# Four tiles' scores in one run, a state tile for each tile, earlier transposes in the second pass, and values before gates in the last head

## The chip, the core and the metric

The kernel runs on one NeuronCore of a Trainium2 chip. The core has a matrix engine (TensorE; PE in the profile, with its weight loads shown apart as PEld), a vector engine (VectorE, DVE), an activation engine (ScalarE, ACT), a general engine (GpSimd, POOL), and a queue that mainly issues DMAs (SyncE, SP). Each runs its own list of instructions in order, and semaphores hold an instruction back until what it needs is there. The working memory (SBUF) holds the operands; TensorE's products go to PSUM, eight banks of 128 x 512 fp32 values.

The metric is the device time of one execution in microseconds, the median over several runs. The kernel before takes 2855.21 us (three runs, 2853.53 to 2857.36).

## What is computed

One layer of a hybrid trunk: a bidirectional gated linear recurrence (HGRN2, 8 heads of 128 x 128 state, 2048 latent tokens, 256 context tokens), then a gated ConvFFN of width 2816. Both are pre-RMSNorm with adaLN. Cut to the part around the change:

```python
def hgrn2_chunk_scan(q, k, v, logf, s0):
    # S_t = diag(f_t) S_{t-1} + k_t v_t^T,  o_t = S_t^T q_t, in chunks of 64
    b = jnp.cumsum(logf, axis=3)
    qe = q * jnp.exp(b - b_ref)
    ke = k * jnp.exp(b_ref - b)
    scores = jnp.where(mask, jnp.einsum('bhnik,bhnjk->bhnij', qe, ke), 0.0)
    o_intra = jnp.einsum('bhnij,bhnjv->bhniv', scores, v)
    kv = jnp.einsum('bhnjk,bhnjv->bhnkv', k * jnp.exp(b_last - b), v)
    s_final, s_start = lax.scan(step, s0, (decay, kv))      # s <- decay * s + kv
    o_inter = jnp.einsum('bhnik,bhnkv->bhniv', q * jnp.exp(b), s_start)
    return o_intra + o_inter, s_final

def hgrn2_mixer(h_ctx, h_lat, w_in, lb, g_gain, w_out, need_ctx):
    # columns of w_in: q | f_fwd | f_bwd | i (values) | g (output gate)
    for d in range(2):                       # both directions, from the context's final state
        oc_d, s_ctx = hgrn2_chunk_scan(..., s0)
        ol_d, _ = hgrn2_chunk_scan(..., s_ctx)
        o_l = o_l + _flip(ol_d, d, 2)
    return (rmsnorm(o_l, g_gain) * jax.nn.silu(g)) @ w_out

lat = lat + g1 * hgrn2_mixer(...)
lat = lat + g2 * conv_ffn(modulate(rmsnorm(lat, norm_g[1]), sh2, sc2), ...)
return rmsnorm(lat, final_g)
```

## The kernel before

**Precision.** A projection is made of three float32r products: each operand is split into a high and a low part (`split`, L76: ScalarE copies the high part, VectorE subtracts), and `acc` (L327) adds high*high, high*low and low*high over the eight blocks of the inner dimension.

**Start.** The adaLN rows for shift and scale come from 64 products with `w_ada` (L202). Their sums are copied to `m2` (L209), two tiles in the pair of places called `raw`, which the loads of weights share, and transposed (L213). Then the first tiles of tokens are modulated and transposed.

**The scan** (`mixer_scan`, L265). Tokens are taken in two halves `g` of 8 tiles of 128; within a half each of the 8 heads is one call of `head(g, h)` (L617), and in it two units `u` of UT = 4 tiles. For each unit there are five projections of 128 x 512 into a tile `z` (three PSUM banks in turn): two gates, the query, the values, the output gate. `gates`, `swish` and `factors` (L361 to L455) turn them into the factors of the recurrence: `kd`, `sd`, `ke`, `qp`, `qi`, `qm`, `km`. `unit_steps` (L496) then gives the rest of the work of a unit:

- `scores(p)`, for the pair p of tiles: transposes of `kd` (`turned`, into the one bank `tr`, copied to `kt` by ScalarE), 24 small products a tile into a bank of `scs`, then two predicated copies and an add on VectorE, to `at`. Each small fp32 product shows as two instructions in the profile, and so does each transposed or 128-column fp32 product of kv and o.
- `outputs(p, v)`: products `kv` of four (L537), products `o` (L543) of the state `Sf` and of `at`, and between them VectorE steps `Sf` to the next tile (L544). So the second tile's product with the state follows a step that itself follows the first tile's product. ScalarE copies `o` and `kv` out, and DMAs put them to DRAM (`stash`) for the backward direction.

The order of this work is written by hand: a clock ticks once for each inner block of a projection (`tick`, L323), three products long, called a slot here, and `at(when, f)` (L313) hangs work onto a later slot, between the products of projections. The lists of numbers in `head` (L655 to L678) are such distances. `head0`'s weights, the context's projections and `make_tok` (the transposes of the next token tiles) use the same clock. Calls give each instruction its priority; the order on an engine is then made by a planner, which may let a later instruction pass one whose inputs it expects late.

In the last half `ada_rest` also makes four adaLN rows on VectorE, one step every 16 slots, and in its last head `gate1` (L603) loads the gate row `g1`, and `out_weight(k)` (L608) loads a block of `w_out`, scales it, and splits it to places 0 to 3, which hold the tokens of the second half until then: places 0 and 1 those of unit 0, places 2 and 3 those of unit 1. Blocks 0 to 3 are made behind out_gate(0), blocks 4 to 7 behind the last head (L703).

**Memory.** SBUF is full. By the sizes of the tiles in the order of the pools, the low end holds the constants, `raw`, `Sf` and `Sb`, the four places, the weights `w`, and then `cxt` (the context's tokens, not used in the second half) from 118.9 to 135.3 KB. The tiles of the second pass grow from the other end, and the lowest of them is `og`, 117.6 to 134.0 KB, then `ghl` and `kq` above it. A tile can be written when the tiles that lay in its place are no longer read.

**The second pass** (`mixer_out`, L846) goes through the tiles backwards. `heads(t)` (L863) loads `kq` of a tile (and uses `og`, loaded by `load_stash(1, t)`), makes the products `oi` with the backward state `Sb` (L877), adds them to o, steps `Sb` (L886) and normalizes by head (L889 to L896). `heads_T(t)` (L899) transposes the result (L906), multiplies by the gate (L908) and splits it to `ghl`. `residual(n, ...)` (L912) multiplies by `w_out`, half of the columns at a time (24 products, 5.5 us), and `norm2` (L948) normalizes the new latents and puts them to DRAM for the FFN. For tile t the loop at L990 calls `heads(t-2)`, `residual(0)` of t, `heads_T(t-1)`, `load_stash(1, t-3)`, `residual(1)` of t and `norm2(t+1)`. `og` and `kq` hold two tiles each, by the tile's parity.

Of the kernel before, what the change touches and what calls it, by code (L numbers as in the profile page):

```python
# [21 lines left out]
D = 1024  # L22
# [23 lines left out]
def body(ctx, tc, a, out):  # L46
# [93 lines left out]
    cxt = hq.tile([128, 2, 2, 2, 4, 128], F32R, name="cxt")  # L140
# [40 lines left out]
    with ExitStack() as c0:  # L181
# [25 lines left out]
        m2 = [rawp.tile([2, 2, 512], F32, name="m2", tag="raw") for _ in range(2)]  # L207
        for n in range(4):
            ada_done = act.activation(m2[n // 2][:, n % 2], mps[n], AF.Copy)  # L209
        m2f = [m.rearrange("p a b -> p (a b)") for m in m2]  # L210
        mt = p0s.tile([128, 16, 2], F32, name="mt")
        for j in range(16):
            pe.transpose(mt[:, j, :], m2f[j // 8][:, j % 8 * 128:(j % 8 + 1) * 128],  # L213
                         ident[0:2, 0:2])
# [50 lines left out]
    def mixer_scan():  # L265
# [19 lines left out]
        for i in range(2):  # L285
            pool.memset(mb[64 * i:64 * i + 64, 0, 64 - 64 * i:128 - 64 * i], 1.0)
        mfu, mbu = [m.bitcast(U32).to_broadcast([128, 2, 128]) for m in (mf, mb)]
        scs = [ps.tile([128, 2, 2, 128], F32, name=f"sc{i}", tag=f"sc{i}", bufs=1)
               for i in range(2)]
        for sc in scs:  # L290
# [5 lines left out]
        ABs = [[fix.tile([128, 2, 128], F32, name=f"AB{i}{d}") for d in range(2)]  # L296
               for i in range(2)]

        TBs = [fix.tile([128, 4, UT, 4], F32, name=f"TB{i}") for i in range(2)]
        TXs = [fix.tile([128, 2, UT, 4], F32, name=f"TX{i}") for i in range(2)]  # L300
        for i in range(2):
# [3 lines left out]
            for d in range(2):  # L305
                pool.memset(ABs[i][d], 0.0)
        count = {"A": 0}
# [68 lines left out]
        def factors(h, u, t0, q):  # L376
# [60 lines left out]
            qm, km = [mid(n, (UT, 4, 32)) for n in ("qm", "km")]  # L437
# [58 lines left out]
        def unit_steps(h, t0, made):  # L496

            kd, sd, ke, qp, qi, qm, km = made
            kts, ats = {}, {}

            def scores(p):

                kts[p] = turned(kd, 2 * p, 2)
                n = count["A"] % 2
                count["A"] += 1
                sc = scs[n]

                def score(i, d, k, kc, q, qc):
                    pe.matmul(sc[32 * kc:32 * kc + 32, i, d, 32 * qc.start:32 * qc.stop], k, q,
                              start=True, stop=True, skip_group_check=True)  # L510

                for i in range(2):
                    s = 2 * p + i
                    for j in range(4):
                        qc = slice(2 - j // 2 * 2, 4 - j // 2 * 2)
                        score(i, 0, km[:, s, j], j, qm[:, s, qc], qc)
                    for d in range(2):
                        for j in range(4):
                            qc = slice(j // 2 * 2, j // 2 * 2 + 2) if j % 2 == 1 - d \
                                else slice(j, j + 1)  # L520
                            score(i, d, ke[:, d, 4 * s + j], j,
                                  qp[:, d, 4 * s + qc.start:4 * s + qc.stop], qc)
                at_ = gp.tile([128, 2, 128], F32, name="at", tag="at", bufs=2)
                af, ab = ABs[n]
                dve.copy_predicated(af, mbu, sc[:, :, 0])
                dve.copy_predicated(ab, mfu, sc[:, :, 1])
# [1000 lines left out]
```

## Time and profile before

| | us |
|---|---|
| median of three runs | 2855.21 |
| profiled execution | 2855.47 |
| its span, first to last instruction | 2853.8 |
| TensorE busy in it | 2764.3 |
| VectorE busy | 1988.9 |
| ScalarE busy | 1158.9 |
| GpSimd busy | 574.6 |

The profile is that of one execution. Times in it count from the start of its span, and are in us unless marked ns. A row of the timeline has start, duration, engine, line of the kernel, operation, output and inputs by the program's names, array size and shape, and the number of instructions merged in it; in brackets is how long the engine had stood idle before and what released it. A row of busy time by stretch has the stretch, its length, then for PE, PEld, DVE, ACT and POOL the busy time and number of instructions, then TensorE's granted clock as a share of the full one, the share of the DMA engines, and GB/s. Matmuls overlap one another, so the distance of their starts tells more than their durations, and a merged row of several can end behind the start of the next row. A row of waits has who waited for whom, the total, how many times, the longest.

### The profile page before, as it was taken

The page shows a single profiled execution, that of the slowest core. Times are in us where ns is not written, and L with a number is a line of the kernel's source. Part 1 is how long each engine was busy: PE and PEld are TensorE (multiplying, and loading weights), DVE is VectorE, ACT ScalarE, POOL GpSimd, SP SyncE. Part 2 cuts the span into 40 slices and gives each one's busy share as a digit, 9 for nine tenths or more (in the row PEclk, how much of TensorE's full clock was granted, in tenths as well). Part 3 has the DMA queues.
Part 4 walks back from the last instruction along what each step waited for, and adds up shares of the span by engine and source line. Part 5 has one row for each costly group of instructions (what it writes and reads, how often), then busy time and mean ns, then how long its engine had stood idle before and what let it go on. Part 6 is the DMA issues. An engine that isn't in the chain of part 4 may idle for free.

```text
span 2853.8 us, 41978 instructions
## 1 busy us (share of the span) xinstructions
PE 2764.3 (97%) x16072; PEld 2277.4 (80%) x16072; DVE 1988.9 (70%) x2900; ACT 1158.9 (41%) x1910; POOL 574.6 (20%) x884
## 2 busy tenths in 40 slices
PE   7999999999999999997999899999999999999999
PEld 3788888888888788886777688888888888878887
DVE  3666555656665666566887787777887777577887
ACT  5524344332232333333565444444444444333343
POOL 2111111111111111111111243433443332000001
PEclk8999999999999999998999999999999999999999
DMA  5213233223532433226778522225422223887663
GB/s 222 66 53 100 82 101 112 82 63 112 170 111 68 141 85 108 89 74 227 265 263 293 223 95 69 82 86 193 179 89 89 85 71 113 305 297 250 205 196 122
DMA packets 223777, 402.18 MB, mean 141 GB/s; under 512 B 29012, under 2 KB 136404, under 8 KB 217816
## 3 DMA queue, kind: packets, MB, share of 16 engines
q1 hardware_dynamic: 220552, 391.24, 41.5%
q10 hardware_dynamic: 3024, 8.26, 0.7%
q8 instruction: 126, 2.06, 0.3%
q14 instruction: 75, 0.61, 0.1%
HBM read 289.04 MB, written 110.38 MB: 140 GB/s over the span
## 4 chain that ended last, share of the span: by engine, by line
PE 71%; DMA 11%; DVE 11%; ACT 3%; issue 2%; POOL 2%; SPq 0%; DVEq 0%; POOLq 0%; ACTq 0%
PE z L332 9%; PE z L334 9%; PE z L333 9%; PE y L1359 3%; PE y L1357 3%; PE y L1358 3%; PE zd L759 3%; PE zc L759 3%; PE zc L761 3%; PE zd L761 3%; PE zd L762 3%; PE zc L762 3%; PE za L761 3%; PE za L762 3%; PE za L759 3%
## 5 line engine op out<-in xcount | busy, mean ns | idle before, releaser
L332 PE MATMUL z<-tok,w 128*128 128x512 f32 x1280 | 516.7, 404 | 0.1
L333 PE MATMUL z<-tok,w 128*128 128x512 f32 x1280 | 505.1, 395 | 0.0
L334 PE MATMUL z<-tok,w 128*128 128x512 f32 x1280 | 501.8, 392 | 0.3 <-DVE w L78 0.3
L78 DVE TENSOR_TENSOR w<-raw,w 128x512 fp32r<-128x512 f32 (+1 forms) x260 | 239.3, 924 | 88.3 <-ACT w L77 86.1
L332 PEld LDWEIGHTS z<-tok,w 128*128 128x128 f32 x1280 | 241.3, 189 | 49.7 <-issue 2.6
L334 PEld LDWEIGHTS z<-tok,w 128*128 128x128 f32 x1280 | 240.9, 188 | 50.0 <-DVE w L78 0.6
L333 PEld LDWEIGHTS z<-tok,w 128*128 128x128 f32 x1280 | 241.6, 189 | 44.3
L77 ACT ACTIVATE w<-raw 128x512 fp32r<-128x512 f32 (+1 forms) x260 | 195.9, 760 | 177.4 <-PE zd L762 77.4
L1357 PE MATMUL y<-wd,mh 128*128 128x512 f32 x600 | 234.9, 392 | 2.8 <-ACT X L1392 2.8
L1359 PE MATMUL y<-wd,ml 128*128 128x512 f32 x600 | 234.6, 391 | 0.6 <-DVE ml L78 0.5
L1358 PE MATMUL y<-wd,mh 128*128 128x512 f32 x600 | 234.4, 391 | 0.0
L78 DVE TENSOR_TENSOR w<-s,w 128x512 fp32r<-128x512 f32 x126 | 121.2, 967 | 53.9 <-ACT w L77 53.1
L759 PE MATMUL zc<-rT,w 128*128 128x512 f32 x352 | 137.1, 390 | 1.2 <-DVE uv L1244 1.0
L762 PE MATMUL zc<-rT,w 128*128 128x512 f32 x352 | 137.0, 389 | 0.0
L761 PE MATMUL zc<-rT,w 128*128 128x512 f32 x352 | 136.9, 389 | 0.0
L1357 PEld LDWEIGHTS y<-wd,mh 128*128 128x128 f32 x600 | 113.3, 189 | 27.2 <-ACT X L1392 3.7
L385 DVE TENSOR_TENSOR_SCAN S<-F,d 128x528 f32<-128x528 f32 (+1 forms) x80 | 91.5, 1144 | 62.2 <-ACT F L368 62.1
L77 ACT ACTIVATE w<-s 128x512 fp32r<-128x512 f32 x126 | 78.2, 627 | 138.8 <-POOL s L815 81.8
L1359 PEld LDWEIGHTS y<-wd,ml 128*128 128x128 f32 x600 | 113.2, 189 | 25.3 <-DVE ml L78 1.4
L1358 PEld LDWEIGHTS y<-wd,mh 128*128 128x128 f32 x600 | 113.3, 189 | 23.4
L759 PE MATMUL za<-rB,w 128*128 128x512 f32 x336 | 130.7, 389 | 0.0
L761 PE MATMUL za<-rB,w 128*128 128x512 f32 x336 | 130.7, 389 | 0.0
(316 smaller groups left out, 6250.5 us busy)
## 6 DMA issues: line engine op xcount, KB each, us to landing
raw<-in_w_up_dram SPq DMA_DIRECT2D x88, 512.0 KB, 3.8
raw<-in_w_in_dram SPq DMA_DIRECT2D x80, 512.0 KB, 3.9
lr<-m SPq DMA_DIRECT2D x49, 512.0 KB, 5.7
m<-r SPq DMA_DIRECT2D x66, 256.0 KB, 4.1
raw<-in_w_ada_dram SPq DMA_DIRECT2D x32, 512.0 KB, 3.7
kq<-stash SPq DMA_DIRECT2D x15, 1024.0 KB, 8.2
og<-stash SPq DMA_DIRECT2D x15, 1024.0 KB, 6.4
u<-in_w_down_dram SPq DMA_DIRECT2D x51, 256.0 KB, 4.0
```

The lines of the kernel that those rows point to most:

```text
L77: act.activation(h, src, AF.Copy)
L78: dve.tensor_tensor(l, src, h.bitcast(F32), OP.subtract)
L332: pe.matmul(z, w[:, 0, k], h, start=k == 0, stop=False, skip_group_check=True)
L333: pe.matmul(z, w[:, 0, k], l, start=False, stop=False, skip_group_check=True)
L334: pe.matmul(z, w[:, 1, k], h, start=False, stop=k == KT - 1, skip_group_check=True)
L385: dve.tensor_tensor_scan(flat(S[:, d]), flat(F[:, d]), flat(d1[:, 0:ns]), 0.0, OP.mult, OP.max)
L759: pe.matmul(o, w[:, 0, k], r[:, :, 0, k], start=start and k == 0, stop=False, skip_group_check=True)
L761: pe.matmul(o, w[:, 0, k], r[:, :, 1, k], start=False, stop=False, skip_group_check=True)
L762: pe.matmul(o, w[:, 1, k], r[:, :, 0, k], start=False, stop=k == 3, skip_group_check=True)
L1357: pe.matmul(z, lh, rh, start=start, stop=False, skip_group_check=True)
L1358: pe.matmul(z, lh, rl, start=False, stop=False, skip_group_check=True)
L1359: pe.matmul(z, ll, rh, start=False, stop=stop, skip_group_check=True)
```

## The change

It has these parts.

1. `m2` at the start goes to four tiles in the places of `q` and `g` instead of the pair `raw`.
2. `scores` takes all four tiles of a unit in one run: one bank of `scs` for each direction instead of one for each pair, masks and sums over four tiles, transposes of the first pair ahead of the products and of the second pair behind them. `at` is four tiles wide. `qm` and `km` get one buffer each instead of two.
3. `outputs(p, v)` becomes `stepped(p)` (kv, the step of the state into a tile `states` for each of the tiles, the stores of kv) and `outputs(p)` (the products o from these states, their stores). They are called as `stepped(0)`, then `outputs(0)` with `stepped(1)`, then `outputs(1)`.
4. The distances in `head` change: scores 16 and 14 slots behind the query (before 20 and 28, and 22 and 28), the three steps at 5, 9, 13 slots behind the values (before two at 6 and 10, or 10 and 16).
5. In the last head the values of unit 1 come ahead of the output gate of unit 0; `gate1` moves from slot 20 to slot 4; blocks 4 to 7 of `w_out` are loaded and scaled at slots 16 to 28 of that head into `wraw`, in the place of `cxt`, and split behind it.
6. In the second pass `heads_T(t-1)` is called ahead of `heads(t-2)` for tiles 14 to 1; tile 15 keeps the old order.

```diff
-        m2 = [rawp.tile([2, 2, 512], F32, name="m2", tag="raw") for _ in range(2)]
+        m2 = [gp.tile([2, 512], F32, name="m2", tag="qg"[n // 2], bufs=2) for n in range(4)]
         for n in range(4):
-            ada_done = act.activation(m2[n // 2][:, n % 2], mps[n], AF.Copy)
+            ada_done = act.activation(m2[n], mps[n], AF.Copy)
...
-        scs = [ps.tile([128, 2, 2, 128], F32, name=f"sc{i}", tag=f"sc{i}", bufs=1)
-               for i in range(2)]
+        scs = [ps.tile([128, UT, 128], F32, name=f"sc{d}", tag=f"sc{d}", bufs=1)
+               for d in range(2)]
...
-            qm, km = [mid(n, (UT, 4, 32)) for n in ("qm", "km")]
+            qm, km = [mid(n, (UT, 4, 32), bufs=1) for n in ("qm", "km")]
...
+            kts, states, vs = [], [], []
+            at_ = gp.tile([128, UT, 128], F32, name="at", tag="at", bufs=2)
+            q_ = act if h == NH - 1 and t0 == NT - UT else sp
+
+            def scores():
+
+                def score(d, s, k, kc, q, qc):
+                    pe.matmul(scs[d][32 * kc:32 * kc + 32, s, 32 * qc.start:32 * qc.stop], k, q,
                               start=True, stop=True, skip_group_check=True)
 
+                kts.append(turned(kd, 0, 2))
+                for s in range(UT):
                     for j in range(4):
                         qc = slice(2 - j // 2 * 2, 4 - j // 2 * 2)
+                        score(0, s, km[:, s, j], j, qm[:, s, qc], qc)
                     for d in range(2):
                         for j in range(4):
                             qc = slice(j // 2 * 2, j // 2 * 2 + 2) if j % 2 == 1 - d \
                                 else slice(j, j + 1)
+                            score(d, s, ke[:, d, 4 * s + j], j,
                                   qp[:, d, 4 * s + qc.start:4 * s + qc.stop], qc)
+                kts.append(turned(kd, 2, 2))
+                for d in range(2):
+                    dve.copy_predicated(ABs[d], masks[d], scs[d])
+                dve.tensor_tensor(at_, *ABs, OP.add)
+
+            def stepped(p):
+
+                if p == 0:
+                    states.append(gp.tile([128, UT - 1, 128], F32, name="states", tag="states",
+                                          bufs=1))
+                kt, v = kts[p], vs[0]
+                st = [Sf[:, h]] + [states[0][:, i] for i in range(UT - 1)] + [Sf[:, h]]
                 kv = ps.tile([128, 2, 2, 128], F32, name="kv", tag="kv")
                 for d in (1, 0):
                     for i in range(2):
+                        pe.matmul(kv[:, d, i], kt[:, i, d], v[:, 2 * p + i], start=True, stop=True)
                 for i in range(2):
+                    s = 2 * p + i
+                    dve.scalar_tensor_tensor(st[s + 1], st[s], sd[:, 1, s:s + 1], kv[:, 1, i],
                                              OP.mult, OP.add)
                 sk = gp.tile([128, 2, 128], F32, name="sk", tag="sk", bufs=2)
...
+            def outputs(p):
+                v = vs[0]
+                st = [Sf[:, h]] + [states[0][:, i] for i in range(UT - 1)]
+                o = ps.tile([128, 2, 128], F32, name="o", tag="o")
+                for i in range(2):
+                    s = 2 * p + i
+                    pe.matmul(o[:, i], qi[:, 1, 4 * s:4 * s + 4], st[s], start=True, stop=False)
+                    pe.matmul(o[:, i], at_[:, s], v[:, s], start=False, stop=True)
+                so = gp.tile([128, 2, 128], F32, name="so", tag="so", bufs=2)
...
+            def second():
+                outputs(0)
+                stepped(1)
+
+            return scores, (vs.append, lambda: stepped(0), second, lambda: outputs(1))
...
         def out_weight(k):
 
-            raw = rawp.tile([128, D], F32, name="raw", tag="raw")
+            if k < 4:
+                raw = rawp.tile([128, D], F32, name="raw", tag="raw")
+            else:
+                if not wraw:
+                    wraw.append(hq.tile([128, 4, D], F32, name="wraw", tag="cxt", bufs=1))
+                raw = wraw[0][:, k - 4]
             sp.dma_start(raw, a["w_out"][k * 128:(k + 1) * 128, :])
             dve.scalar_tensor_tensor(raw, raw, vec[:, V_GN:V_GN + 1], g1s[0], OP.mult, OP.mult)
-            split(w_out_part("h", k), w_out_part("l", k), raw)
+            if k < 4:
+                split(w_out_part("h", k), w_out_part("l", k), raw)
...
             if first:
                 gate(0)
-                query(0, (24, 40))
+                query(0, 24)
...
             gate(0)
-            query(0, (20, 28))
+            query(0, 16)
             gate(1)
-            query(1, (22, 28))
-            value(0, (6, 10))
-            out_gate(0)
+            query(1, 14)
+            value(0, (5, 9, 13))
             if g == 1 and h == NH - 1:
+                value(1, (9, 13, 17))
+                out_gate(0)
                 for k in range(4):
                     at(clock[0] + 2 * k, lambda k=k: out_weight(k))
-            value(1, (10, 16))
+            else:
+                out_gate(0)
+                value(1, (5, 9, 13))
             out_gate(1)
...
                 if g == 1 and h == NH - 1:
-                    at(clock[0] + 20, gate1)
+                    at(clock[0] + 4, gate1)
+                    for k in range(4, KT):
+                        at(clock[0] + 4 * k, lambda k=k: out_weight(k))
                 head(g, h)
+        run(1 << 30)
         for k in range(4, KT):
-            out_weight(k)
-        run(1 << 30)
+            split(w_out_part("h", k), w_out_part("l", k), wraw[0][:, k - 4])
...
+            if t and t < NT - 1:
+                gs.append(heads_T(t - 1, ogs.pop(0)))
             if t > 1:
                 ogs.append(heads(t - 2, steps))
...
             residual(0, lat, *g)
-            if ogs:
+            if t == NT - 1:
                 gs.append(heads_T(t - 1, ogs.pop(0)))
```

100 lines of the change are left out of this document (34 added, 66 removed).

## The prediction

> **What bounds the kernel now.** I read the page first, then busy time by stretch, then who TensorE waits for, then the timeline where it stands still.
>
> ```profile
> span 2853.8 us, 41978 instructions
> PE 2764.3 (97%) x16072; PEld 2277.4 (80%) x16072; DVE 1988.9 (70%) x2900; ACT 1158.9 (41%) x1910; POOL 574.6 (20%) x884
> ...
> 0.00:84.00 84.00, 61.86 (x239) 33.45 (x240) 29.40 (x74) 45.67 (x82) 17.70 (x47) 0.84 0.50 189
> 84.00:1285.00 1201.00, 1184.92 (x8982) 989.59 (x8981) 751.91 (x1177) 409.06 (x688) 194.69 (x444) 1.00 0.31 96
> 1285.00:1315.00 30.00, 15.69 (x73) 13.90 (x71) 20.25 (x38) 9.16 (x20) 2.08 (x3) 0.66 0.78 276
> 1315.00:1585.00 270.00, 253.59 (x1310) 210.38 (x1311) 206.71 (x426) 150.35 (x342) 34.72 (x32) 0.98 0.75 263
> ```
>
> The stretches are the start, the scan of 16 heads, the passage to the second pass, and the second pass (first four columns: length, PE, PEld, DVE). TensorE sets the time nearly everywhere; VectorE has 449 us free in the scan but only 63 of 270 in the second pass. The change doesn't touch what follows 1585. So gains can only come from TensorE's idle time (22 us at the start, 16 in the scan, 14 in the passage, 16 in the second pass) and from products that take more than their columns.
>
> **Score runs.** TensorE's timeline at a pair's products and at a score run:
>
> ```profile
> 1196.46 1.05 PE L537 MATMUL kv<-v,kt 128*128 128x128 f32 x8
> 1197.35 0.39 PE L543 MATMUL o<-Sf,qi 128*128 128x128 f32 x2
> ...
> 1198.25 0.39 PE L333 MATMUL z<-tok,w 128*128 128x512 f32 x1
> 1198.48 0.40 PE L334 MATMUL z<-tok,w 128*128 128x512 f32 x1
> 1199.21 0.49 PE L543 MATMUL o<-Sf,qi 128*128 128x128 f32 x2 [0.34 <-DVE Sf L544]
> ...
> 1249.66 0.40 PE L334 MATMUL z<-tok,w 128*128 128x512 f32 x1
> 1249.90 0.60 PE L462 MATMUL tr<-ident,kd 128*128 128x128 f32 x4
> 1250.42 0.32 PE L509 MATMUL sc<-qm,km 128*32 128x64 f32 x8
> ...
> 1251.13 0.50 PE L332 MATMUL z<-tok,w 128*128 128x512 f32 x1
> 1251.48 0.40 PE L333 MATMUL z<-tok,w 128*128 128x512 f32 x1
> ...
> L464 ACT ACTIVATE kt<-tr 128x512 f32<-128x512 f32 x72 | 42.9, 595 | 92.4 <-PE tr L462 92.1
> ```
>
> A z product starts 0.23 us behind the one before (1198.25, 1198.48), so a slot, the three products of one k, is 0.68 us. Eight kv instructions take 0.89 (1196.46 to 1197.35), 0.11 each.
> From z at 1249.66 to the second z at 1251.48 are 1.82 us; without two z (0.46) and four transposes (0.44, of kv's width) a run of 48 score instructions costs 0.92. Of it 0.08 lies before the first score and 0.12 in the slow first z (0.35 for 0.23). There are two runs per unit and 32 units. In one run the second half adds its scores, 1250.42 to 1251.13 or 0.71 at most, and saves the 0.20 at the edges; some of the 0.71 is the tail before the z, too. I take 0.64 for the half: 0.28 x 32 = 9 us gained. Upper bound 11 (the half adds 0.58). Lower bound: the second four transposes use the one tr bank and wait for ScalarE's copy of the first four (L464, 0.60 us). The scores between, over 1.1 us, hide it; without that cover 0.6 x 32 = 19 is lost, net -10.
>
> The Trainium skill ("TensorEngine Tiling (Array Packing)", Key Properties) says that changing the tiling mode drains TensorE. By it all of the edge (0.20 and the tail) goes once per run saved, 11 us instead of 9, and the total would be 2 us lower.
>
> VectorE's predicated copies and add become three wide ones for six a unit. With its 449 us free, worth 0.
>
> **State tiles, and products o after them.**
>
> ```profile
> PE o L543 <- DVE Sf L544: 8.7, 13, 3.8
> ...
> PEld o L543 <- DVE Sf L544: 14.0, 19, 4.2
> ```
>
> Who TensorE and its weight loads wait for in the scan (total us, times, longest). The last o products follow a z or two behind the rest and wait until VectorE has stepped Sf: above, 1198.48 to 1199.21 is 0.73 for 0.23. With a state of its own per tile, o runs four slots (2.7 us) after its step. Of the waits in the scan, 14.0 us by the weight loads and 8.7 by the products, I take 13 as gone; bounds 8.7 and 14. New is `stepped(0)` at slot 5, three slots (2.0 us) behind the transposes of v. ScalarE's copy of v, as wide as kt's (0.60), must fit, with 1.4 us for what stands before it. Behind that kv stand all z products. I give back 2 us; bounds 0 and 10 (0.3 x 32). Interrupting z four times a unit becomes three; z to kv costs nothing beyond the columns, so 0.
>
> Scores come earlier, 16 and 14 slots after the query. They need the last factor; the unit in which it is latest:
>
> ```profile
> 968.42 0.59 ACT L372 ACTIVATE q<-z 128x512 f32<-128x512 f32 x1
> 978.66 0.68 DVE L454 TENSOR_TENSOR ke<-ke,rt 128x512 f32<-128x512 f32 x1
> ```
>
> It ends 10.9 us behind the query, against 16 slots or 10.9 us, and 14 slots plus the runs of v (0.44) and kv (0.89), 10.8. Nothing waits. Single buffers for qm and km are written after those scores. The stores of sk move ahead of those of so on SP, with no more issues than before. The first head's slots shift by a few with the same products: 0, within two slots (1.4 us) either way.
>
> Scan: -9 - 13 + 2 = **-20**; ends: -25 (11 + 14) and +11 (10 lost at the scores, 10 at kv, 8.7 gained).
>
> **The passage.**
>
> ```profile
> 1284.62 0.39 PE L334 MATMUL z<-tok,w 128*128 128x512 f32 x1
> ...
> 1288.69 1.28 DVE L612 SCALAR_TENSOR_TENSOR raw<-raw,vec,g 128x1024 f32<-128x1024 f32 x1 [0.71 <-DMA raw<-in_w_out_dram]
> 1290.29 0.80 PE L543 MATMUL o<-Sf,qi 128*128 128x128 f32 x2 [3.72 <-DVE Sf L544]
> 1292.63 0.33 SPq L611 DMA_DIRECT2D raw<-in_w_out_dram  x1
> 1294.49 0.33 SPq L858 DMA_DIRECT2D kq<-stash  x1
> 1299.64 1.23 DVE L78 TENSOR_TENSOR wo<-raw,wo 128x1024 fp32r<-128x1024 f32 x1 [1.12 <-ACT wo L77]
> 1300.57 3.60 PE L877 MATMUL oi<-Sb,kq 128*128 128x128 f32 x16 [4.79 <-DMA kq<-stash]
> 1308.65 3.75 PE L877 MATMUL oi<-Sb,kq 128*128 128x128 f32 x16 [4.49 <-DMA kq<-stash]
> 1315.09 0.50 PE L917 MATMUL y<-wo,ghl 128*128 128x512 f32 x1 [0.73 <-ACT ghl L77]
> ```
>
> From the last z (1284.62) to the first y: 30.5 us. VectorE stands behind the loads of w_out, so Sf and o are late; the load of kq stands on SP behind the last such load. Afterwards values go before gates, so all but 8 instructions of o (0.9 us) stand ahead of the last z; before, four tiles' kv and o (32 of 0.11, 3.5 us) came after it. So 2.6 us of work move ahead, no gain. Four loads and four products of w_out (4 x 1.28 = 5.1 us) move into the head's first half, under VectorE's free time in the scan; uncovered they cost 5.1. gate1 and the bias row it takes through the raw pair move up 16 slots past weight loads on SP, which run ahead of their use.
> The catch: these four blocks now lie in the place of cxt, which og's place overlaps by the pool sizes. og can't load until they are split, and their split waits for the last z (place 3) and for the splits of weights 2 and 3, whose raws come only after out_gate(0). VectorE then has six splits (1.23) and two products (1.28), 10 us from about the last z. og leaves at +7 to +10 and lands 6.4 later (below). Before, y came 14.5 behind the first oi, 4.5 of it the wait for the next kq, and og is needed 2 us into these 10: y at +21 to +24. With the later end, 30.5 - 2.6 - 24 = **-4**; ends -9 (og early) and +2.
>
> **Second pass.**
>
> ```profile
> og<-stash SPq DMA_DIRECT2D x15, 1024.0 KB, 6.4
> PE y L917 <- ACT ghl L77: 9.3, 6, 3.3
> PE tp L109 <- DVE xn L929: 3.3, 3, 2.5
> PE tp L109 <- DVE rs L73: 2.8, 3, 1.8
> 1455.57 1.03 PE L109 MATMUL tp<-ident,xn 128*128 128x128 f32 x8
> 1458.07 1.28 ACT L896 ACTIVATE og<-og,rs 128x128 f32<-128x128 f32 x4 [1.25 <-POOL rs L74]
> ```
>
> Moving `heads_T(t-1)` ahead of `heads(t-2)` lets ghl and og's reload come one residual (5.5 us) earlier: the 9.3 us that y waits go. But the transposes now need og when the norm's transposes end, 1456.6, and it is finished at 1459.35: 2.7 us late at today's pace. VectorE's work per tile is 13 us against TensorE's 16 (207 and 254 over 16 tiles), and og's reload, on which VectorE waits today, comes earlier. So I expect most of the lateness to go and some to stay: -9 + 7 = **-2** (0.5 us at each of 14 tiles). Ends: -15 (all rows above) and +29 (2.7 x 14 less 9).
>
> **The start.**
>
> ```profile
> PE mt L213 <- ACT m L209: 8.1, 1, 8.1
> 41.76 1.15 ACT L100 ACTIVATE x<-x,rs 128x1024 f32<-128x1024 f32 x1 [0.91 <-POOL rs L74]
> 42.81 2.00 ACT L209 ACTIVATE m<-mps 2x512 f32<-2x512 f32 x4
> ```
>
> m2 no longer takes the raw pair. Its copies stand on ScalarE behind four x tiles; whether they pass these is an order that no row shows. Between 0 and -8: I take **-1**, since the row ahead of them is x, not a weight.
>
> **Sum.** The profiled execution took 2855.5, its span 2853.8; the median is 2855.2, the same. 2855.5 - 20 - 4 - 2 - 1 = 2828.5, so **2828**.
>
> **Rivals.** (a) Slower: the transposes of each of 14 tiles wait the 2.7 us and the products behind them can't pass; what y waited is only moved. 2855.5 - 25 + 38 = 2868.5. It decides from 1.8 us a tile (25 / 14). For it: the row at 1458.07; against: og's earlier reload.
> The Trainium skill ("TensorE: Matmul & The Clock Gate", "Step-by-step: what each phase is for") says that only weight loads are pulled ahead and matmuls stay in order. By that rule nothing fills the wait and rival (a) has its full price; the trace agrees at 1290.29, where nothing passed for 3.72 us.
> (b) The change doesn't do what it says: z products slip into the score run, or o's wait comes back as a wait of kv on v and sk. The scan gains 4, the rest as above with nothing in the passage: 2855.5 - 4 - 2 - 1 = 2848.5. For it: the present order already has o two z late, which the calls don't say.
> (c) All idle time of the second pass (15), 9 in the passage and 4 at the start go: 2855.5 - 20 - 28 = 2807.
>
> **Chances.** Forecast (2815 to 2842) 0.58, (a) 0.11, (b) 0.17, (c) 0.14. A measurement of this kernel can't tell 0.2% (5.7 us, 2849.5 to 2860.9) from no change. Faster: 0.58 + 0.14 + 0.12 of (b) = 0.84; same 0.05 of (b) + 0.02 of (a) = 0.07; slower 0.09. The range reaches to (c) and (b), 2806 to 2851, leaving out 0.11 of (a) and 0.07 beyond the others.
>
> **What would show it.** One run of 96 scores per unit; no o waiting for a state in the scan; the scan's stretch 20 us shorter with the same products. kq issued before the last z and og's load as the last wait ahead of the first y; y's waits for ghl gone, the wait of transposes on og small. Wrong if z starts between scores, if kv's waits exceed 10 us, or if transposes wait over 1.8 us a tile.

## The result and the profile after

Beside the kernel before on the same chip, the changed kernel took **2828.96 us** (median of 4 runs, 2827.11 to 2832.5) against 2854.37 (4 runs): ratio 0.9911, 95% interval 0.9894 to 0.9928. In a later comparison (run 2 below) it took 2823.94 against 2853.05, ratio 0.9889 (0.9874 to 0.9905). The forecast was 2828, with 2806 to 2851 around it. The total was right; its terms for the scan and the second pass were not.

First the page of the changed kernel, then busy time by stretch (columns as in the prediction). Scan, passage and second pass start and end at the same distances from the first z, the last z, and the first and last y as those of before; the start's stretch is 83.15 us long then (84 before) and the rest, counted to 2830 and 2853, 1270.78 (1268 before).

```profile
span 2830.8 us, 41935 instructions
PE 2742.5 (97%) x16072; PEld 2274.9 (80%) x16072; DVE 1981.7 (70%) x2804; ACT 1151.0 (41%) x1910; POOL 560.1 (20%) x882
...
83.15:1281.91 1198.76, 1177.20 (x9009) 994.44 (x9008) 746.57 (x1089) 406.64 (x692) 182.44 (x444) 0.99 0.31 98
1281.91:1304.41 22.50, 9.35 (x49) 8.46 (x48) 17.23 (x31) 7.84 (x16) 2.94 (x3) 0.70 0.81 289
1304.41:1559.22 254.81, 246.19 (x1310) 209.50 (x1311) 209.74 (x429) 149.75 (x347) 34.39 (x32) 0.99 0.75 278
```

| stretch | predicted | first profile | second profile |
|---|---|---|---|
| start | -1 | -0.9 | -0.9 |
| scan | -20 | -2.2 | -5.7 |
| passage | -4 | -7.5 | -7.4 |
| second pass | -2 | -15.2 | -14.4 |
| rest | 0 | +2.8 | -1.1 |

The second profile is the repeat's (first z 73.9, last z 1278.0, first y 1301.1, last y 1539.6, span 2824.2). The rest, which the change doesn't touch, came out longer in one and shorter in the other, so in one profile a stretch can't be told to better than 2 or 3 us, and the scan to less than that ("One clock" below). The 2.6 us of kv and o that move ahead of the last z count in the scan here and counted in the passage in the prediction: like for like the scan gave 5 to 8 us where 20 were expected, the passage 5 where 4 were.

**The scan.** TensorE's busy time fell by 7.7 us there (1184.92 to 1177.20) though 27 more instructions stand in it; its idle time rose from 16.1 to 21.6. Who TensorE and its weight loads (last row) wait for in the scan of the changed kernel (total us, times, longest):

```profile
PE tr L471 <- ACT vt L465: 13.0, 5, 3.1
PE o L555 <- DVE states L533: 2.3, 2, 1.3
...
PE kv L530 <- ACT v L472: 1.3, 1, 1.3
...
PEld o L555 <- DVE states L533: 2.9, 2, 1.7
```

The waits of o are all but gone, as intended (8.7 and 14.0 us before). In their stead the transposes of v wait 13.0 us, which was 2.5 before: three of 2.7 (8.2 in all), one of 3.1 and a shorter one. The first of the three, on TensorE, SP and ScalarE of the changed kernel, in order of time:

```profile
275.48 0.32 PE L501 MATMUL sc<-qm,km 128*32 128x64 f32 x8
...
280.03 0.60 PE L109 MATMUL tp<-ident,xt 128*128 128x128 f32 x4
...
285.64 0.33 SPq L160 DMA_DIRECT2D tok<-stg  x1
291.24 1.06 ACT L97 ACTIVATE junk<-xt 128x1024 f32<-128x1024 f32 x1 [6.28 <-DMA tok<-stg]
292.29 0.58 ACT L465 ACTIVATE vt<-z 128x512 f32<-128x512 f32 x1
292.93 0.66 PE L471 MATMUL tr<-ident,vt 128*128 128x128 f32 x4 [2.75 <-ACT vt L465]
```

and the same place before the change:

```profile
276.53 0.60 PE L109 MATMUL tp<-ident,xt 128*128 128x128 f32 x4
277.06 0.32 PE L509 MATMUL sc<-qm,km 128*32 128x64 f32 x8
...
281.55 0.33 SPq L160 DMA_DIRECT2D tok<-stg  x1
284.49 1.06 ACT L97 ACTIVATE junk<-xt 128x1024 f32<-128x1024 f32 x1 [1.43 <-DMA tok<-stg]
288.34 0.60 ACT L470 ACTIVATE vt<-z 128x512 f32<-128x512 f32 x1 [2.22 <-PE z L334]
```

The second transposes of an x tile (`tp` of `xt`) stood right ahead of a score run; now the run (`sc`) stands four slots ahead of them. That tile's second half is copied out 4 us later (285.64 for 281.55; 1 us of it is the two kernels' offset at this place), and takes 5.6 us to land where it took 2.9. (On SP a load of weights left 0.6 us ahead of this copy, and 4.4 us ahead of it before the change; whether that slowed it is not shown.) The squares of the next x tile write their by-product into the copy's place (`junk` and `stg` share it), so ScalarE stands 6.28 us until the copy has landed, and the copy of the values stands behind it.

A score run of 96, on TensorE:

```profile
1260.90 0.39 PE L329 MATMUL z<-tok,w 128*128 128x512 f32 x1
...
1263.68 0.40 PE L328 MATMUL z<-tok,w 128*128 128x512 f32 x1
```

From z to second z are 2.78 us; without two z (0.46) and eight transposes (0.89) the run costs 1.43. Two runs cost 1.84, so 0.41 a unit is saved, 13 us over 32 units, where 0.28 and 9 were expected. Added up in the same way over all score runs of the scan, the cost falls from 64 us before to 54 in the first profile and 52 in the second, so 10 to 12 are gained. Two units of the 32 have no run of 96: in the first head and near 1050 us the scores stand in pieces between other products. (The section on the kernel speaks of 24 small products a tile: they are 24 instructions, of 12 products.)

**The passage**, on SP, VectorE and TensorE of the changed kernel:

```profile
1284.85 1.29 SPq L577 DMA_DIRECT2D stash<-g  x3
1287.12 0.38 SPq L876 DMA_DIRECT2D kq<-stash  x1
1287.10 3.48 DVE L78 TENSOR_TENSOR wo<-wraw,wo 128x1024 fp32r<-128x1024 f32 x3
1290.61 0.32 SPq L876 DMA_DIRECT2D og<-stash  x1
1295.53 0.69 DVE L899 TENSOR_TENSOR og<-og,oi 128x512 f32<-128x512 f32 x1 [0.43 <-DMA og<-stash]
1304.50 0.64 PE L935 MATMUL y<-wo,ghl 128*128 128x512 f32 x1 [1.22 <-ACT ghl L77]
```

og's load leaves as the last split out of cxt's place ends, 9.1 us behind the last z (1281.53); y follows at +23.0, where +24 was expected.

**The second pass.** Who TensorE, then VectorE waits for in the changed kernel, and one row of VectorE before:

```profile
PE tp L924 <- ACT og L914: 6.0, 5, 1.3
PE y L935 <- ACT ghl L77: 1.2, 1, 1.2
PE tp L924 <- DVE og L912: 1.2, 1, 1.2
...
DVE og L899 <- DMA og<-stash: 1.1, 1, 1.1
```

```profile
DVE og L881 <- DMA og<-stash: 17.0, 8, 3.7
```

The transposes' new waits are the 7 us of the prediction. But VectorE's 17.0 us of waiting for og are all but gone, and with them the waits of the norm's transposes (3.3 and 2.8 us before, 0.5 now) as well as y's. Idle time fell by 7.8 us and busy time by 7.4 with the same 1310 products (253.59 to 246.19): behind longer waits TensorE had run slower. Its granted clock was at half for 10.2 us of the second pass before and for 3.4 after, which makes 3.4 of the 7.4; the other 4 were not traced. One such place before, behind waits of 2.5 us (until 1376.65) and 1.6 us (until 1381.04), by length, busy time (instructions), clock, DMA share and GB/s:

```profile
1382.00:1386.00 4.00, 4.00 (x12) 0.57 0.78 254
```

### The profile page after: what moved, and what is told of

The parts are those of the page before. It is cut to its first block, busy times and chain, and to the rows that moved or that the text cites. A ratio compares the mean times of both kernels' runs of the same rounds, so it can differ in the third digit from the quotient of the medians.

```text
span 2830.8 us, 41935 instructions
## 1 busy us (share of the span) xinstructions
PE 2742.5 (97%) x16072; PEld 2274.9 (80%) x16072; DVE 1981.7 (70%) x2804; ACT 1151.0 (41%) x1910; POOL 560.1 (20%) x882
## 4 chain that ended last, share of the span: by engine, by line
PE 74%; DMA 11%; DVE 9%; issue 2%; ACT 2%; POOL 1%; SPq 1%; DVEq 0%; POOLq 0%; ACTq 0%
PE z L327 9%; PE z L329 9%; PE z L328 9%; PE zd L777 3%; PE zd L779 3%; PE zd L780 3%; PE zc L777 3%; PE zc L780 3%; PE zc L779 3%; PE za L777 3%; PE za L780 3%; PE za L779 3%; DMA lr<-m 2%; PE kv L530 2%; PE y L1377 2%
```

## The experiments

Times are medians; ratios are to the kernel before in the same comparison, with 95% intervals. Line numbers in rows are each kernel's own.

**One clock.** Behind some waits TensorE's granted clock falls to half for 3.4 us or more (last section), and how often differs from run to run. So scans are compared here with that taken out. The third column adds up, over slices of 1 us from the first z to the last, the time at half clock. The fourth is the length less half of it, an estimate: z products start 0.43 us apart at half clock and 0.23 else (295.16 and 295.59 in the first profile, and 1198.25 and 1198.48 before).

| scan | length, us | at half clock | at one clock |
|---|---|---|---|
| before; run 3, which has the same scan | 1209.8; 1210.1 | 7; 6 | 1206; 1207 |
| changed; again; run 2; run 2 again | 1207.5; 1204.1; 1201.2; 1197.5 | 26; 21; 13; 6 | 1195; 1194; 1195; 1195 |
| run 1; run 7 (x tiles moved up) | 1201.8; 1203.2 | 7; 9 | 1198; 1199 |
| run 4 (two score runs) | 1213.9 | 18 | 1205 |
| run 5 (one place for the state) | 1210.7 | 10 | 1206 |
| run 9 (a place of its own) | 1198.5 | 15 | 1191 |

The four profiles of the changed scan differ by 10 us in length and by 1 at one clock. At one clock the change took 12 us off the scan, 14 to 15 with the 2.6 us that moved into it; the half clocks took 7 to 9 of them back in the first two profiles.

**1. The x tile's slots.** In the changed kernel, the second x tile of a head moved up by four slots, so that its second transposes stand ahead of the score run again:

```
-                            at(clock[0] + 8 + 44 * n + 8 * i, f)
+                            at(clock[0] + 8 + 40 * n + 8 * i, f)
```

> The changed kernel with the second x tile of each of heads 2 to 5 of the first half moved up by four slots (its three steps at 48, 56 and 64 slots instead of 52, 60 and 68), so that the transposes of its second half stand ahead of the score run again and not behind it. Theory: in the changed kernel that tile's copy to memory leaves late, the next tile's squares wait for its place on ScalarE, the copy of the values stands behind them, and the transposes of v wait 2.75, 2.69 and 2.72 us in three heads. Then these three waits go, 8 us, the waits of these transposes in the scan fall from 13.0 to about 5 us, and the kernel takes about 2821 us (8 less than the changed kernel). Rival: ScalarE is late with the copy of the values for its own place in the order, because a run of 96 scores has both copies of kt behind it; then the waits stay within 1 us of each other and the time stays at 2829.

2823.48 us, ratio 0.9899 (0.9884 to 0.9914). Waits of TensorE in its scan:

```profile
PE kv L530 <- ACT v L472: 5.2, 4, 1.3
PE tr L457 <- ACT kt L459: 4.8, 5, 1.9
PE tr L471 <- ACT vt L465: 3.3, 2, 3.1
```

The cause holds: the three waits are gone. The price doesn't: waits of kv for v (5.2 for 1.3) and of transposes for the one tr bank (4.8 for 1.6) came in their place, most of them in the same heads, and the time can't be told from the changed kernel's two medians (2829.0, 2823.9). At one clock the scan is even 3 to 4 us longer; what the move gave back is half clocks, 7 us for 21 and 26.

**2. The second pass's transposes back**, in the changed kernel:

```
-            if t and t < NT - 1:
-                gs.append(heads_T(t - 1, ogs.pop(0)))
...
-            if t == NT - 1:
+            if ogs:
                 gs.append(heads_T(t - 1, ogs.pop(0)))
```

> The changed kernel with the transposes of the second pass back in their old place, behind the first residual. Theory: the order of the transposes alone makes the 15 us that the second pass became shorter (from 253 to 238 us between its first and last y); then og is loaded late again, VectorE waits for it some 17 us as before, and the kernel takes 2829 + 13 = about 2842 us. Rival, as predicted: the order is worth 2 us, and the rest of the 15 comes from how the passage leaves the queues; then it takes about 2831.

2832.02 us, ratio 0.9937 (0.9913 to 0.9960), which alone would fit the rival. The profile did not: the second pass was 252 us long again, and scan and rest happened to be 6 us shorter each than in the first profile of the changed kernel. So both were run again, side by side.

> The changed kernel itself, again, beside the next run on the same chip. Between its first and last y the profile should show 238 us again; the scan's stretch (first to last z) was 1207.6 us in its first profile and 1201.2 and 1205.0 in two profiles of kernels that differ from it only behind the scan, so 1201 to 1208 is expected, and about 2829 us in all.

> The changed kernel with the transposes of the second pass in their old place, as in the second run, again. Theory: the second pass is 252 us long against 238, and the rest of the kernel is the same but for what varies from run to run, so that in the same comparison it takes 10 to 14 us longer than the changed kernel: 2839 to 2843. Rival: the kernel's part behind the second pass, which waits for vectors and stores of the second pass, gives a part of the 14 back, and the difference is 3 to 7 us: 2832 to 2836.

The changed kernel took 2823.94, ratio 0.9889 (0.9874 to 0.9905); with the transposes back it took 2835.08, ratio 0.9936 (0.9924 to 0.9949): 11 us more. First and last y products of the kernel before, the changed one (first profile), the one with the transposes back (second run) and that of run 3, one row each:

```profile
L917 PE MATMUL y<-wo,ghl x256: 387/389/796, 1315.1 to 1567.6; 128*128 128x512 f32 x128
```

```profile
L935 PE MATMUL y<-wo,ghl x256: 389/389/639, 1304.5 to 1541.8; 128*128 128x512 f32 x128
```

```profile
L935 PE MATMUL y<-wo,ghl x256: 387/389/792, 1294.8 to 1546.7; 128*128 128x512 f32 x128
```

```profile
L917 PE MATMUL y<-wo,ghl x256: 387/389/500, 1314.4 to 1550.3; 128*128 128x512 f32 x128
```

**3. Only the second pass's transposes moved**, in the kernel before:

```
+            if t and t < NT - 1:
+                gs.append(heads_T(t - 1, ogs.pop(0)))
             if t > 1:
                 ogs.append(heads(t - 2, steps))
...
-            if ogs:
+            if t == NT - 1:
                 gs.append(heads_T(t - 1, ogs.pop(0)))
```

> The kernel before with nothing but the transposes of the second pass moved up. Theory: the second pass alone gains 13 to 15 us, the rest is untouched: about 2854 - 14 = 2840. Rival, as predicted: 2 us, 2852. Second rival: the transposes wait 2.7 us at every tile because this kernel's passage leaves og's loads as late as they were, and it takes 2860 or more.

2838.79 us, ratio 0.9952 (0.9938 to 0.9967), 14 us less. The four rows give 252.5, 237.3, 251.9 and 235.9 us: the order of these transposes alone makes the 15. With half of their time at half clock taken off (10, 3, 10 and none) they come to 247, 236, 247 and 236, so 12 of it are work and waits and 3 the clock.

**4. Two score runs a unit**, in the changed kernel:

```
-            def scores():
+            def scores(p):
...
-                kts.append(turned(kd, 0, 2))
-                for s in range(UT):
+                kts.append(turned(kd, 2 * p, 2))
+                for s in range(2 * p, 2 * p + 2):
...
-                at(clock[0] + after, scores)
+                for p in range(2):
+                    at(clock[0] + after + 2 * p, lambda p=p: scores(p))
```

> The changed kernel with the scores of a unit in two runs of 48 again, two slots apart; the predicated copies stay wide, behind the second run. Theory: each run costs 0.89 to 0.91 us beyond its neighbours' columns and the run of 96 costs 1.43, so that 0.36 to 0.39 us a unit come back, 32 units: about 2829 + 12 = 2841. By the prediction's 0.28 a unit it would be 2838. Rival: the edges of a run cost nothing that the longer run doesn't pay elsewhere; then it stays at 2829.

2834.02 us, ratio 0.9937 (0.9916 to 0.9958): 5 and 10 us above the changed kernel's medians. The interval overlaps that of the changed kernel's first comparison, so the time alone doesn't decide. Its scan, 73.8 to 1287.7, is 6 and 10 us longer, and 10 at one clock, near the 12 of the theory: joining the runs is worth about 10 us.

**5. One place for the state**, in the changed kernel; a pair's o stands with its kv again:

```
+                    inner = qi[:, 1, 4 * s:4 * s + 4]
+                    pairs = [(inner, Sf[:, h]), (at_[:, s], v[:, s])]
+                    for n, (l, r) in enumerate(pairs[::-1] if i else pairs):
+                        pe.matmul(o[:, i], l, r, start=n == 0, stop=n == 1)
-                    dve.scalar_tensor_tensor(st[s + 1], st[s], sd[:, 1, s:s + 1], kv[:, 1, i],
+                    dve.scalar_tensor_tensor(Sf[:, h], Sf[:, h], sd[:, 1, s:s + 1], kv[:, 1, i],
```

> The changed kernel with one place for the state again: a tile's o products are issued with its kv, ahead of the state's next step, as before the change; the rest stays. Theory: the second o of a pair waits for VectorE's step again, over 12 us of such waits in the scan against 2.3 in the changed kernel, and the kernel takes 2829 + 12 = about 2841. Rival: these waits stand where values are late anyway, and only take their place; then the waits for the values fall by as much and the time stays within 3 us of 2829.

2834.35 us, ratio 0.9936 (0.9919 to 0.9952), again 5 and 10 us above. Waits of TensorE and its weight loads in its scan:

```profile
PE tr L471 <- ACT vt L465: 12.9, 5, 3.0
PE o L533 <- DVE Sf L534: 7.9, 7, 1.6
...
PEld o L533 <- DVE Sf L534: 11.5, 12, 1.9
```

The waits of o return (2.3 and 2.9 in the changed kernel) and v's don't fall, so the rival is out. At one clock the scan is 11 us longer, near the 12 of the theory.

**6. The last head as before** (gates ahead of values, all of w_out through the raw pair), in the changed kernel:

```
-                value(1, (9, 13, 17))
                 out_gate(0)
                 for k in range(4):
                     at(clock[0] + 2 * k, lambda k=k: out_weight(k))
+                value(1, (5, 9, 13))
...
-        run(1 << 30)
         for k in range(4, KT):
-            split(w_out_part("h", k), w_out_part("l", k), wraw[0][:, k - 4])
+            out_weight(k)
+        run(1 << 30)
```

> The changed kernel with the last head as it was before: gates ahead of the values in its second unit, all eight blocks of w_out through the raw pair, the last four loaded behind the head. Theory: the passage from the last z to the first y is 23.0 us long in the changed kernel because four blocks are loaded early and og waits only for their splits; without that it is 30 us again and the kernel takes 2829 + 7 = about 2836. Rival: the passage is set by the loads of og and kq, which stand behind the stores of the last gates on SP, and is short for that order; then it stays within 2 us of 2829.

2828.73 us, ratio 0.9909 (0.9894 to 0.9923): no difference that can be told. The passage (last z 1278.0, first y 1303.2) is 25.2 us long, 2.2 more than with the change and 5 less than before. Rows of SP and VectorE:

```profile
1285.72 0.38 SPq L868 DMA_DIRECT2D og<-stash  x1
...
1294.32 0.68 DVE L891 TENSOR_TENSOR og<-og,oi 128x512 f32<-128x512 f32 x1
```

og's load leaves at +7.7, earlier than with the change (+9.1); VectorE, with the late blocks ahead of it, gets to og at +16.3 instead of +14.0. But 16 more instructions of kv and o stand behind the last z here (24 for 8), 1.8 us at 0.11 that the changed kernel has in its scan. Like for like, early blocks and early values together are worth 0.4 us, which is why the time doesn't show them. So the 5 us that the passage gained came with the other parts of the change; which of them brought it was not taken apart.

**7. Sums first.** In the changed kernel TensorE stands still for 1.26 us ahead of the transposes of og at every second tile. On VectorE, POOL, ScalarE and TensorE:

```profile
1359.62 1.67 DVE L904 SCALAR_TENSOR_TENSOR Sb<-Sb,decb,kq 128x128 f32<-128x128 f32 x6
1361.20 1.29 DVE L907 TENSOR_REDUCE ss<-oi 128x4 f32<-128x512 f32 x2
1363.40 1.65 POOL L74 TENSOR_TENSOR rs<-rs,mhalf 128x8 f32<-128x8 f32 x1 [4.72 <-DVE rs L73]
1365.08 1.28 ACT L914 ACTIVATE og<-og,rs 128x128 f32<-128x128 f32 x4 [5.87 <-POOL rs L74]
1365.88 1.06 PE L924 MATMUL tp<-ident,og 128*128 128x128 f32 x8 [1.26 <-ACT og L914]
```

The sums stand behind six steps of Sb that nobody waits for yet. With run 1's slots, and in `heads`:

```
+            for hs, oi in zip(q4s, ois):
+                dve.tensor_reduce(ss[:, hs], oi, AX.X, OP.add)
+            if between:
+                between.pop(0)()
+            rms_scale(rs, ss, NH, 128)
             for h in range(NH):
                 dve.scalar_tensor_tensor(Sb[:, h], Sb[:, h], decb[:, h, t:t + 1],
                                          kq[:, h, 0], OP.mult, OP.add)
-            for hs, oi in zip(q4s, ois):
...
```

> The changed kernel with the x tiles moved up as in the first run, and in the second pass the sums of squares taken ahead of the eight steps of Sb. Theory: in the changed kernel the transposes of every second tile wait 1.43 us for the scaled og, which waits for the sums, which stand behind five or six steps of Sb on VectorE (1.4 to 1.7 us); with the sums first these waits go, the second pass falls from 237 to about 228 us and the kernel takes 2823 - 9 = about 2814. Rival: the tiles are bound by the POOL power and the scaling behind it (1.65 and 1.28 us), or the later Sb makes the next products oi wait; then it stays at 2823.

**2814.54 us**, ratio 0.9861 (0.9845 to 0.9878), 9 us below run 1. First and last y, and who og's transposes wait for from the passage to the end of the second pass:

```profile
L935 PE MATMUL y<-wo,ghl x256: 387/389/796, 1298.8 to 1526.6; 128*128 128x512 f32 x128
```

```profile
PE tp L924 <- DVE og L912: 1.7, 1, 1.7
```

227.8 us for 237.3, and the waits at every second tile are gone.

**8. Other blocks early.** With the sums first, the four blocks whose places come free with the first unit's last z lie in cxt's place; the other four go through the raw pair, two of them loaded on POOL's queue, which also stores the last gates:

```
-            if k < 4:
+            if k >= 4:
                 raw = rawp.tile([128, D], F32, name="raw", tag="raw")
...
-            sp.dma_start(raw, a["w_out"][k * 128:(k + 1) * 128, :])
+            (pool if k > 5 else sp).dma_start(raw, a["w_out"][k * 128:(k + 1) * 128, :])
```

> The run before it (sums first), and in the last head the blocks of w_out swapped: the first four lie in the place of cxt and are split during the last gates, since their places come free with the first unit's last z; the last four go through the raw pair, two of them loaded on POOL's queue, and the last unit's gates are stored from POOL's queue. Theory: og can't load before the splits out of cxt's place; when these no longer wait for the last z, og's load leaves about 6 us earlier, and the passage falls from 23 to about 17 us: 2814 - 6 = about 2808. Rival: the four late blocks (two products and four splits behind the last z, 7.5 us of VectorE) come between og and its products, and the passage stays at 22 to 24 us.

2822.12 us, ratio 0.9887 (0.9873 to 0.9902): 8 us slower, the passage 27.7. og's load did leave at +2.3, but on VectorE:

```profile
1286.62 1.28 DVE L623 SCALAR_TENSOR_TENSOR raw<-raw,vec,g 128x1024 f32<-128x1024 f32 x1 [6.99 <-DMA raw<-in_w_out_dram]
1290.51 1.28 DVE L623 SCALAR_TENSOR_TENSOR raw<-raw,vec,g 128x1024 f32<-128x1024 f32 x1 [2.60 <-DMA raw<-in_w_out_dram]
```

The late blocks (issued at 1278.21 and 1279.34) land 8 and 11 us later, and both VectorE and ScalarE stand in order behind them: TensorE waits 7.15 us for ScalarE's copy for kq, until 1293.24. Whether the loads of kq and og beside them or POOL's queue made them late is not shown. Then with the last two blocks in the places of hm and stg, and no load left behind the last z:

```
+            elif k < 6:
+                raws[k] = rawp.tile([128, D], F32, name="raw", tag="raw")
+            else:
+                raws[k] = xp.tile([128, D], F32, name="xraw", tag=("hm", "stg")[k - 6], bufs=1)
```

> The sums-first kernel with the first four blocks of w_out in cxt's place as in the run before, the next two in the raw pair and the last two in the places of hm and stg, so that all eight are loaded and scaled ahead of the last z and only four splits stand behind it. Theory: in the run before og's load left 2.3 us behind the last z and not 9, but two blocks loaded late (they landed 10 and 14 us behind the last z, beside kq's and og's loads), and the copies for kq and the products of Sb stood behind their splits. With no late load, VectorE is done with the splits some 6 us behind the last z, the passage is 16 to 18 us against 22.1, and the kernel takes 2814.5 - 5 = about 2809. Rival: hm and stg lie where kq or og lie, or the loads take as long side by side as before; then the passage stays at 21 to 24 us and the time at 2814.

2816.63 us, ratio 0.9870 (0.9857 to 0.9884). The passage is 18.5 us (1276.8 to 1295.3) against 22.1, as the theory had it, but the second pass takes 3.8 us more than in run 7 (first y 1295.3, last 1527.4), at its last tiles: given back, and no gain that can be told.

**9. A place of its own.** In the changed kernel, with the sums first and the x tiles at their slots:

```
-        junk = xp.tile([128, D], F32, name="junk", tag="stg", bufs=1)
+        junk = xp.tile([128, D], F32, name="junk", tag="hm" if t >= HT else "stg", bufs=1)
```

> The changed kernel (x tiles at their slots, not moved up) with the sums first in the second pass, and with the squares of the second half's x tiles written into the place of hm and not of stg, so that ScalarE does not wait there for the copy of the tile before to land. Moving the tiles up by four slots took the three waits of v's transposes away, but waits of kv for v and of the transposes of kd for the copies came in their stead (5.2 and 4.8 us against 1.3 and 1.6), and the waits of the scan came to 20.4 us as against 21.3. Theory: the wait hangs on the place alone; now v's transposes wait under 5 us in the scan, nothing comes in its stead, the waits of the scan come to 13 us, and the kernel takes 2814.5 - 5 = about 2809. Rival: ScalarE's work is late there in any order, the waits turn up at another instruction again, and it takes 2814 to 2818 like the sums-first kernel.

**2812.42 us**, ratio 0.9854 (0.9837 to 0.9872), the fastest, though not to be told from run 7. Waits of TensorE in its scan:

```profile
PE kv L530 <- ACT v L472: 4.6, 4, 1.3
PE tr L471 <- ACT vt L465: 4.5, 2, 2.9
```

The three waits hung on the shared place: the x tile stands where it stood in the changed kernel, and v's copy is no longer late. Of their 8 us, 3 came back as waits of kv for v, since ScalarE scales the x tile ahead of v's copy. At one clock the scan is 3 to 4 us shorter than the changed kernel's and 8 shorter than run 7's. That the time shows only 2 of these 8 is due to the second pass, 234.2 us for 228.3: in this profile og's transposes wait for ScalarE again at four tiles (4.0 us), though the sums come first. Why is not shown.

## Why the prediction was right in sum and wrong in its terms

**Scan, -20.** The mechanism of the o waits was right: 13 expected; 6 went by the products' rows and 11 by the weight loads'. So was that of the score runs (9 expected, 10 to 12 measured: the edge was larger, though two units stay in pieces) and of kv's wait for v (2 expected, 1.3). What failed is the step "Scores come earlier ... Nothing waits." It asked whether the scores' factors are ready, and not what stood between the old and the new place of the run: an x tile's transposes, their copy out, and behind that ScalarE's place for the values. The prediction followed the moved step past SP and TensorE, not past ScalarE. The three waits cost 8.2 us, and in the first two profiles a half clock behind each, 1.7 us apiece: 13 together, about the 12 to 15 that the scan fell short. Run 9 shows that the shared place made them. The prediction had no term for the clock at all, though a wait of 3.8 us before the change (until 986.67) was followed by 3.4 us at half clock. Rival (b) had the scan's size, not its mechanism: z slipped between the scores of two units only, and o's wait did not come back at kv.

**Passage, -4.** The order was right: og waits for the splits out of cxt's place and y comes at +23 for +24. Two details were wrong. kq did not leave before the last z but 5.6 us behind it, after the gates' stores on SP; that cost nothing here, since VectorE still waited 0.43 us for og behind it. And the early blocks, named as the reason, are not it: run 6 takes them back, and like for like 0.4 of the 5 us go with them. So the size was right and the reason not; what made the passage shorter stays open.

**Second pass, -2.** The step that failed is "-9 + 7 = -2". Both numbers came true (y's waits 10.0 to 1.2 us; new waits of the transposes 6.0 + 1.2). But the sum credited only the wait that the edit names. og's reload comes some 12 us earlier against the tiles' products, where the prediction had one residual, 5.5 us. That also ended nearly all of VectorE's 17.0 us of waiting, and with it the norm's late transposes; those rows stood in the prediction and were left for rival (c). Runs 2 and 3 show that the order alone did it.

**Start, -1.** The stretch is 0.9 us shorter, but that this is the change's doing is not shown. Two of the four copies of m now stand ahead of the last x tile's squares and two behind them, TensorE's wait for them became longer (9.5 us for 8.1), and the first z comes at 72.9 to 74.6 us in the profiles with this start, at 74.4 and 74.8 in the two with the old one.

So one term was 12 to 15 us too large and another 13 too small, and the sum hit by chance. The range held because rivals with either term were in it.

## What to carry over

When a step moves, list what it now stands ahead of on every engine, and follow that work to the buffer it fills: a shared scratch place turns a copy that lands late into a stall of the next engine. Where an edit ends a wait of an engine that feeds others (here VectorE for og), credit every wait behind that engine, not only the one that the edit aims at. And a total that is right proves no term: compare stretch by stretch, and take the time at half clock out first, or two profiles of the same scan differ by 10 us.

## What the hardware showed beside this

**A wait can cost more than its length.** Length, busy time (instructions), granted clock, DMA share and GB/s behind the wait shown above in the changed kernel, and behind the same wait in the second run with the transposes back, whose scan has the same products:

```profile
294.00:296.00 2.00, 2.00 (x7) 0.59 0.00 0
296.00:298.00 2.00, 2.00 (x11) 0.56 0.00 0
```

```profile
294.00:298.00 4.00, 4.00 (x107) 1.00 0.14 37
```

In the one TensorE runs at half clock for 3.4 us, in the other not at all, and so it was at the other two of the three waits. That scan was 10 us shorter (74.3 to 1271.8, 1197.5 us, against 1207.5); it has 20 us less at half clock, and half of that is the whole difference. The idle times were 2.75 and 2.65 us. Over the scans of eleven of the profiles, 27 of 37 waits of TensorE between 1.9 and 3.8 us had a half clock behind them, and none of those between 1.0 and 1.85. The Trainium skill ("TensorE: Matmul & The Clock Gate", "Part 1: The HAM clock gate") gives the half clock after an idle window of about 3.4 us that runs free of the kernel. The chance in it agrees with these runs; the length doesn't, since these waits were shorter.
